# The first layer's experts add their results by accumulating indirect transfers to device memory instead of one-hot products

## Chip, cores and metric

One core of a Trainium2 chip runs the whole program; the core's engines are TensorE (PE), VectorE (DVE), ScalarE (ACT), GpSimd (POOL) and SyncE (SP), and sixteen DMA engines move data between device memory and on-chip memory. The metric is the device time of one execution in microseconds; a kernel's time is the median of several runs. The trace comes from one further execution that the hardware profiler recorded.

## The reference

Two layers work on 512 latent tokens and 256 context tokens of width 1024, in float32. Each layer mixes tokens (four groups of heads, one output projection, gated residual) and then runs 16 routed experts. The experts are what matters here:

```
def expert_choice_ffn(x, router_w, wg, wu, wd):
    bn, n, _ = x.shape
    cap = CAPACITY_FACTOR * n // N_EXPERTS
    aff = jax.nn.softmax(jnp.einsum('bnd,de->bne', x, router_w).astype(jnp.float32), axis=-1)
    gate, idx = lax.top_k(aff.transpose(0, 2, 1), cap)
    bidx = jnp.arange(bn)[:, None, None]
    xg = x[bidx, idx]
    hid = jax.nn.silu(jnp.einsum('becd,edf->becf', xg, wg)) * jnp.einsum('becd,edf->becf', xg, wu)
    o = jnp.einsum('becf,efd->becd', hid, wd) * gate[..., None].astype(x.dtype)
    return jnp.zeros_like(x).at[bidx, idx].add(o)
...
        x = x + g2 * expert_choice_ffn(...)
        if not last:
            xc = xc + cg2 * expert_choice_ffn(...)
```

Each expert chooses `cap` tokens: 64 of the 512 latent ones, 32 of the 256 context ones. A token can be chosen by several experts, but an expert lists a token once. The first layer runs the experts on both kinds of tokens with the same weights, the second layer on the latent tokens alone. Each expert has three 1024 x 1024 matrices (gate, up, down), 4 MB each, 201 MB a layer.

## The kernel before

On-chip memory is one slab of 49984 words per partition that `Arena` hands out. `Stream` (`st`) holds the weight transfers of both layers in a fixed order. It issues the next one on SP's queue as soon as less than `st.limit` words are held, so each product that frees a chunk (`st.done`) pumps the next transfer. An expert matrix is four chunks of 2048 words per partition (1024 KB, `CUTS`). `AHEAD` and `BESIDE` (lines 41 and 42) set the limit by stage and layer.

Ahead of the experts of a layer, `wout_unit` computes the output projection and adds it to the residual `X` (six tiles of 128 tokens), `rows_out` (L1397) stores the finished columns of `X` to `rows` in device memory, `willing` and `route` find each expert's tokens, and `fetch` (L1463) gathers 128 rows at a time from `rows` by an indirect transfer on GpSimd's queue: two experts' latent tokens, or four experts' context tokens. `turned` scales and transposes what was gathered.

In the first layer `experts_both` (L1804) goes through the experts. For expert e it runs `gate` of e+1, then `down` of e, then `up` of e+1, each by `both_mm` (L1647): for every chunk, `lat_mm` (L1602, 16 matmul records a chunk) and `ctx_mm` (L1610, 8 records). TensorE's order is the order written here (`in_turn`); the other engines' orders are set by a scheduler that simulates the program. `out_lat` and `out_ctx` multiply the results by the routing weights and the layer's gate, into `o`, a tile of 128 rows that two experts (latent) or four (context) fill together.

When a tile is full, `scatter(r, g)` (L1723) adds it to `X`. `mark` builds a matrix that has a one where a row of `o` belongs to a token; `o` is split into a high and a low part, and each `part` multiplies both with the one-hot matrix (L1733 and L1734, one matmul record each) and adds the bank to a 128 x 512 piece of `X` on VectorE (L1736). A latent group has 8 parts and a context group 4; with 8 and 4 groups that is 80 parts in the first layer. They wait in `todo`, and `both_mm` takes up to two of them after a chunk of weights:

```
                if c in at:
                    at[c]()
                else:
                    for _ in range(min(much, len(todo))):
                        todo.popleft()()
```

The last 12 parts follow the last expert. Then the second layer starts with the `X` that is still on the chip: `norm1` squares its rows (L717), VectorE scales them (L722), and TensorE turns them (L610). `X` is also stored to `x1` (L1923), from where the second layer reads it again before its output projection (L1290). The second layer's experts (`experts_latent`) use `scatter` too, without `todo`.

Of the kernel before, what the change touches and what calls it, by code (L numbers as in the profile page):

```python
# [28 lines left out]
NE = 16  # L29
# [10 lines left out]

AHEAD = ((16384, 20480), (16384, 24576), (28672, 40960))
BESIDE = (26624, 34816)
MORE = (4096, 8192)
# [183 lines left out]
def hybrid_kernel(ctx: ExitStack, tc: tile.TileContext, T, out):  # L227
# [35 lines left out]
    def small(n, name, dt=F32, bufs=4, p=128):  # L263
        return smp.tile([p, n], dt, name=name, tag=name, bufs=bufs)
# [248 lines left out]
    def latest(engine):  # L513
        return next(i for i in reversed(nc.cur_bb.bb.instructions) if i.engine == engine)
# [22 lines left out]
    def layer(l):  # L537
# [751 lines left out]
        for s in (slice(0, 512), slice(512, 1024)):  # L1289
            sp.dma_start(X.v[:, 0:4, s], tiles(T["x"])[:, :, s] if cx else x1.rearrange("t p f -> p t f")[:, 0:4, s])  # L1290
            if cx:
                sp.dma_start(X.v[:, 4:6, s], tiles(T["ctx"])[:, :, s])
# [104 lines left out]
        def rows_out(r, a, b):  # L1397

            sp.dma_start(rows[r][:, a:b].rearrange("(t p) f -> p t f", p=128),
                         X.v[:, 4 * r:4 * r + (4 >> r), a:b])  # L1400

        def route(lat):
# [52 lines left out]
            return icol, ii, gcol  # L1455

# [39 lines left out]
        def mark(r, g):  # L1496

            n = 512 if r == 0 else 256
            m = ohm()
            dve.tensor_scalar(m.r[:, 0:n], iota.v[:, 0:n], rt[r][0][:, g:g + 1], None, OP.is_equal)  # L1500
            return m
# [88 lines left out]
        if cx:  # L1590
            setbanks(G=[0, 1, 2], C=[3, 4], T=[5, 6, 7])
            kinds["X"] = kinds["T"]
        else:
            setbanks(G=[0], U=[1], D=[3], T=[5, 6], X=[7, 2, 4])
        OO, OC = {}, {}

# [47 lines left out]

        todo = deque()

        def both_mm(e, wn, xl, xc, at, much=2):  # L1647

            B, Cb = bank("G"), bank("C")
            for c, (k0, nk) in enumerate(CUTS):  # L1650
                w = st.get(("exp", l, e, wn, k0))
                lat_mm(B, xl(), w, k0, nk)
                ctx_mm(Cb, xc(), w, k0, nk)
                st.done(("exp", l, e, wn, k0))
                if c in at:
                    at[c]()
                else:
                    for _ in range(min(much, len(todo))):
                        todo.popleft()()
            return B, Cb  # L1660
# [31 lines left out]
        def out_lat(e, B):  # L1692
            gc = rt[0][2]
            if e % 2 == 0:
                OO[e // 2] = orr()
            o = OO[e // 2].v
            p0 = (e % 2) * 64
            for n in range(2):
                s = slice(n * 64, n * 64 + 64)
                dve.scalar_tensor_tensor(o[p0:p0 + 64, n * 512:(n + 1) * 512], B[s, :], gc[s, e:e + 1],  # L1700
                                         G2.v[s, 0, n * 512:(n + 1) * 512], OP.mult, OP.mult)

        def out_ctx(e, Cb):
            if e % 4 == 0:
                OC[e // 4] = orc()
            o = OC[e // 4].v
            gc = rt[1][2]
            p0 = (e % 4) * 32
            a, b = halves(Cb, gc[64:128, e:e + 1])
            dve.scalar_tensor_tensor(b, a, gc[0:64, e:e + 1], b, OP.mult, OP.add)  # L1710
            for n in range(2):
                s = slice(n * 32, n * 32 + 32)
                dve.tensor_tensor(o[p0:p0 + 32, n * 512:(n + 1) * 512], b[s, :],
                                  G2.v[s, 1, n * 512:(n + 1) * 512], OP.mult)

        def down(e, hT):
# [5 lines left out]

        def scatter(r, g):  # L1723

            m = mark(r, g)
            o = (OO if r == 0 else OC)[g]
            n = 512 if r == 0 else 256
            ol = o.split()

            def part(t, s, oh):  # L1730
                B = bank("X")
                lh = m.r[:, t * 128:(t + 1) * 128]
                pe.matmul(B, lh, oh.r, start=True, stop=False)  # L1733
                pe.matmul(B, lh, ol[:, s], start=False, stop=True)  # L1734
                xs = X.v[:, 4 * r + t, s]
                dve.tensor_tensor(xs, xs, B, OP.add)  # L1736

            for f in range(2):
                s, oh = slice(f * 512, (f + 1) * 512), ohr()
                act.activation(oh.r, o.v[:, s], AF.Copy)  # L1740
                dve.tensor_tensor(ol[:, s], o.v[:, s], oh.v, OP.subtract)
                for t in range(n // 128):
                    if cx:
                        todo.append(lambda t=t, s=s, oh=oh: part(t, s, oh))
                    else:
                        part(t, s, oh)

# [56 lines left out]
        def experts_both():  # L1804

            nonlocal iota, ohm, ohr
            hT, wait = {}, {}
# [17 lines left out]
            with in_turn():  # L1825
# [3 lines left out]
                for e in range(NE):  # L1829
# [14 lines left out]
                    B, Cb = both_mm(e, "down", lambda: x, lambda: y, {})  # L1844
                    while todo:
                        todo.popleft()()
# [12 lines left out]
                    if e + 1 < NE:  # L1859
# [9 lines left out]
                        B, Cb = first(e + 1, "up", spread(fs))  # L1869
                while todo:  # L1870
                    todo.popleft()()

        def experts_latent():
# [3 lines left out]
            for e in range(NE - 1):  # L1877
# [28 lines left out]
                if e % 2:  # L1906
                    scatter(0, e // 2)

# [5 lines left out]
        if not cx:  # L1914
            finish(NE - 1, hl)
        for r in (xtr, xgr, et, h1r, ht, orr, ohr, ohm) + ((xtc, h2r, hcr, htc, orc) if cx else ()):
            r.free()
        G2.free()
        ar.tight = False
        iota.free()  # L1920
# [118 lines left out]
```

## Time and profile before

| | before |
|---|---|
| median of 3 runs | 1978.82 us (1976.78 to 1978.9) |
| the profiled execution | 1984.42 us |
| its span, first to last instruction | 1982.3 us |
| TensorE matmul busy | 1825.0 us, 92% |
| VectorE busy | 897.6 us, 45% |
| ScalarE busy | 653.7 us, 33% |
| GpSimd busy | 228.4 us, 12% |
| HBM read, written | 513.40 MB, 10.52 MB |
| mean rate | 264 GB/s |

Times in rows count from the start of the span. "x" is a number of instructions, and what stands in brackets or behind an arrow is what an engine waited for before an instruction. The first layer's experts run from about 540 to 1106 us, the second layer's from about 1525 us to the end.

### The profile page before, as it was taken

The numbers are of one execution on the slowest core, as the hardware profiler recorded it, in microseconds if no ns is written. First come the engines' busy times: TensorE is split into PE (matmuls) and PEld (weight loads), VectorE is DVE, ScalarE is ACT, GpSimd is POOL, SyncE is SP. The second block draws the span as 40 slices with busy tenths as digits, with TensorE's granted clock in tenths as the row PEclk, the third lists the DMA queues.
The fourth block names the chain that finished last, engine by engine and source line by source line (L and its number), as shares of the span: only waits on it lengthen the run. The fifth ranks groups of instructions, "written<-read, shape, count | busy, mean of one in ns | idle before, by whom it ended". The sixth has DMA issues, their size and how long they took to land.

```text
span 1982.3 us, 31560 instructions
## 1 busy us (share of the span) xinstructions
PE 1825.0 (92%) x13037; PEld 1022.3 (52%) x13037; DVE 897.6 (45%) x1881; ACT 653.7 (33%) x1390; POOL 228.4 (12%) x191
## 2 busy tenths in 40 slices
PE   6999988989899999999999799998898999888888
PEld 3886787679533333333333488696694333222323
DVE  3758564533523434434434575864534233223322
ACT  2456544532322322331221345644521211111101
POOL 0432033101100000000000044132110000000000
PEclk9999999979899999999999899998998999999999
DMA  9116135532699999999998122425737999999997
GB/s 341 55 49 200 43 115 174 195 138 86 224 409 407 386 344 364 372 351 357 351 359 298 59 64 99 144 94 196 280 104 287 422 421 421 422 422 422 422 422 293
DMA packets 156542, 525.97 MB, mean 265 GB/s; under 512 B 12240, under 2 KB 42864, under 8 KB 132336
## 3 DMA queue, kind: packets, MB, share of 16 engines
q1 hardware_dynamic: 153664, 514.00, 68.2%
q0 software_dynamic: 2736, 9.97, 1.3%
q8 instruction: 102, 1.67, 0.3%
q14 instruction: 40, 0.33, 0.0%
HBM read 513.40 MB, written 10.52 MB: 264 GB/s over the span
## 4 chain that ended last, share of the span: by engine, by line
PE 33%; DMA 15%; DVE 4%; ACT 2%; issue 1%; SPq 1%; POOL 0%; ACTq 0%; DVEq 0%; POOLq 0%
PE banks L1602 15%; DMA ar<-in_exp_w_gate 4%; DMA ar<-in_exp_w_down 4%; DMA ar<-in_exp_w_up 4%; PE banks L1610 3%; PE banks L1332 2%; DMA ar<-in_w_in 2%; PE banks L633 1%; PE banks L702 1%; PE banks L644 1%; PE banks L1733 1%; PE banks L463 1%; PE banks L1734 1%; SPq L1035 1%; PE banks L1486 0%
## 5 line engine op out<-in xcount | busy, mean ns | idle before, releaser
L1602 PE MATMUL banks<-ar,ar 128*32 128x512 f32 (+1 forms) x4576 | 714.1, 598 | 32.9 <-DMA ar<-in_exp_w_down 14.0
L1602 PEld LDWEIGHTS banks<-ar,ar 128*32 128x32 f32 (+1 forms) x4576 | 194.6, 119 | 457.2 <-issue 379.0
L1610 PE MATMUL banks<-ar,ar 128*32 128x512 f32 x1536 | 201.2, 598 | 0.1
L633 PE MATMUL banks<-ar,ar 128*128 128x256 f32 x1344 | 175.8, 287 | 2.1 <-DVE ar L812 1.6
L633 PEld LDWEIGHTS banks<-ar,ar 128*128 128x128 f32 x1344 | 166.7, 193 | 7.2 <-issue 2.6
L1332 PE MATMUL banks<-ar,ar 128*128 128x256 f32 x960 | 137.7, 299 | 2.4 <-ACT ar L1228 1.3
L1332 PEld LDWEIGHTS banks<-ar,ar 128*128 128x128 f32 x960 | 125.8, 201 | 4.4 <-ACT ar L1228 2.4
L1736 DVE TENSOR_TENSOR ar<-ar,banks 128x512 f32<-128x512 f32 x136 | 87.4, 683 | 66.1 <-PE banks L1734 65.8
L1610 PEld LDWEIGHTS banks<-ar,ar 128*32 128x32 f32 x1536 | 50.8, 111 | 115.8 <-issue 107.9
L1466 POOL DMA_INDIRECT ar<-rows,icoli x19 | 18.4, 970 | 769.7 <-ACT ar L1491 455.4
L1700 DVE SCALAR_TENSOR_TENSOR ar<-banks,gcol,ar 64x512 f32<-64x512 f32 x62 | 46.5, 750 | 126.7 <-PE banks L1602 126.0
L411 ACT ACTIVATE ar<-banks 128x512 f32<-128x512 f32 x32 | 19.1, 597 | 256.3 <-PE banks L1602 256.3
L1491 ACT ACTIVATE ar<-banks,modT,modA 128x128 f32<-128x128 f32 x84 | 31.5, 458 | 169.4 <-PE banks L1483 138.4
L576 POOL TENSOR_TENSOR ar<-ar,ar 128x2048 fp32r<-128x2048 f32 x14 | 64.8, 4626 | 177.6 <-ACT ar L575 177.6
L463 PE MATMUL banks<-ar,S 128*32 128x256 f32 x768 | 66.3, 418 | 19.6 <-DMA ar<-in_ada_w 18.7
L911 ACT ACTIVATE ar<-banks,mx 128x768 f32<-128x768 f32 (+1 forms) x80 | 65.2, 819 | 31.1 <-DVE mx L908 28.5
L702 PE MATMUL banks<-ar,ar 128*128 128x512 f32 (+1 forms) x288 | 71.6, 395 | 3.8 <-DVE ar L603 2.0
L908 DVE TENSOR_REDUCE mx<-banks 128x1 f32<-128x768 f32 (+1 forms) x80 | 66.6, 846 | 15.2 <-PE banks L903 12.1
L414 DVE SCALAR_TENSOR_TENSOR ar<-banks,ar 128x512 f32<-128x512 f32 x32 | 21.9, 683 | 112.0 <-ACT ar L413 112.0
L1671 DVE TENSOR_TENSOR ar<-banks,ar 64x512 f32<-64x512 f32 x32 | 21.8, 680 | 95.1 <-ACT ar L1616 95.1
L644 PE MATMUL banks<-ar,ar 128*128 128x512 f32 (+1 forms) x288 | 62.2, 370 | 2.3 <-ACT ar L820 2.2
L1679 DVE COPY ar<-banks 128x512 f32<-128x512 f32 x32 | 22.1, 691 | 91.0 <-PE banks L1677 91.0
(343 smaller groups left out, 2541.7 us busy)
## 6 DMA issues: line engine op xcount, KB each, us to landing
ar<-in_exp_w_gate SPq DMA_DIRECT2D x128, 1024.0 KB
ar<-in_exp_w_up SPq DMA_DIRECT2D x128, 1024.0 KB
ar<-in_exp_w_down SPq DMA_DIRECT2D x124, 1024.0 KB
ar<-in_ada_w SPq DMA_DIRECT2D x96, 512.0 KB
ar<-in_w_in SPq DMA_DIRECT2D x18, 1024.0 KB
ar<-in_w_out SPq DMA_DIRECT2D x8, 1024.0 KB
ar<-in_exp_w_down SPq DMA_DIRECT2D x7, 512.0 KB
ar<-in_rpb SPq DMA_DIRECT2D x8, 384.0 KB
```

The costliest lines, as they stand in the source:

```text
L463: pe.matmul(B[32 * q:32 * q + 32, 0:n], S[:, k, :], w[:, q * n:(q + 1) * n], start=k == 0, stop=k == 7)
L576: pool.tensor_tensor(lo, raw, hi.v, OP.subtract)
L633: pe.matmul(B[:, tt * 256:(tt + 1) * 256], a.r[:, k, t * 128:(t + 1) * 128], b[:, k, :], start=n == 0, stop=n == 23)
L644: pe.matmul(B[:, 0:n1 - n0], b[:, k, c * 128:(c + 1) * 128], a.r[:, k, n0:n1], start=n == 0, stop=n == 23)
L702: pe.matmul(PS[:, t, s], x.r[:, k, t * 128:(t + 1) * 128], w, start=k == 0 and i == 0, stop=k == 7 and i == 2)
L908: dve.tensor_reduce(mx, s, AX, OP.max, negate=True)
L911: act.activation(e, s, AF.Exp, bias=mx, accum_out=sm)
L1332: pe.matmul(B, a[:, c, t * 128:(t + 1) * 128], b[:, k, :], start=i == 0, stop=i == 23)
L1602: pe.matmul(B[n * 64 + j:n * 64 + j + p, :], xt[:, k, j:j + p], w[:, k - k0, n * 512:(n + 1) * 512], start=k == 0, stop=k == 7)
L1610: pe.matmul(B[j:j + 32, :], xt[:, k, :], w[:, k - k0, n * 512:(n + 1) * 512], start=k < 2, stop=k > 5)
L1700: dve.scalar_tensor_tensor(o[p0:p0 + 64, n * 512:(n + 1) * 512], B[s, :], gc[s, e:e + 1], G2.v[s, 0, n * 512:(n + 1) * 512], OP.mult, OP.mult)
L1736: dve.tensor_tensor(xs, xs, B, OP.add)
```

## The change

The first layer keeps its residual in device memory during the experts. `x1` is replaced by `xs_`, one tensor of 512 rows and one of 256 rows. `rows_out` stores each piece to `rows` and to `xs_`, and `X` is freed after the routing. Each expert's result is now one tile of its own (64 latent rows or 32 context rows), and `give` adds it to the chosen rows of `xs_` by an indirect transfer with an add, issued on GpSimd's queue: 32 transfers. After the last expert, `X` is allocated again and loaded from `xs_` by six transfers, and the second layer's later read of `X` takes `xs_[0]`. `route` computes the row numbers that this needs. The deque, the one-hot matrices and the table `iota` of the first layer go; the limits on weights ahead rise in the first layer. The second layer's experts keep the one-hot products.

```diff
-AHEAD = ((16384, 20480), (16384, 24576), (28672, 40960))
-BESIDE = (26624, 34816)
+AHEAD = ((16384, 20480), (16384, 24576), (32768, 40960))
+BESIDE = (32768, 34816)
...
-    x1 = drp.tile([6, 128, D], F32, name="x1")
+    xs_ = [drp.tile([n, D], F32, name="xs%d" % n) for n in (NL, NCX)]
...
         def rows_out(r, a, b):
-            sp.dma_start(rows[r][:, a:b].rearrange("(t p) f -> p t f", p=128),
-                         X.v[:, 4 * r:4 * r + (4 >> r), a:b])
+            for d in (rows[r], xs_[r]) if cx else (rows[r],):
+                sp.dma_start(d[:, a:b].rearrange("(t p) f -> p t f", p=128), X.v[:, 4 * r:4 * r + (4 >> r), a:b])
...
+            to = None
+            if cx:
+                tof = small(16, "tof%d" % r, bufs=1)
+                dve.tensor_tensor(tof[0:cap], dif[0:cap], ia[0:cap], OP.add)
+                to = small(16, "to%d" % r, I32, bufs=1)
+                dve.tensor_copy(to[0:cap], tof[0:cap])
...
         rt[0] = route(True)
+        if cx:
+            X.free()
...
         def out_lat(e, B):
             gc = rt[0][2]
-            if e % 2 == 0:
+            if cx or e % 2 == 0:
                 OO[e // 2] = orr()
             o = OO[e // 2].v
-            p0 = (e % 2) * 64
+            p0 = 0 if cx else (e % 2) * 64
...
+            if cx:
+                give(0, e, o)
+
+        def give(r, e, o):
+            n = 64 >> r
+            pool.indirect_dma_start(out=xs_[r], out_offset=bass.IndirectOffsetOnAxis(
+                ap=rt[r][3][0:n, e:e + 1], axis=0), in_=o[0:n], in_offset=None, compute_op=OP.add)
...
         def out_ctx(e, Cb):
-            if e % 4 == 0:
-                OC[e // 4] = orc()
-            o = OC[e // 4].v
+            o = orc().v
...
+            give(1, e, o)
...
                     out_lat(e, B)
                     out_ctx(e, Cb)
-                    if e == 1:
-                        iota = Buf(ar, (512,))
-                        sp.dma_start(iota.v, T["iota"])
-                        ohm, ohr = Rot(ar, (512,), 2), Rot(ar, (512,), 4)
-                    if e + 1 == NE:
-                        kinds["X"][0] = [5, 6, 7, 0, 1, 2, 3, 4]
-                    if e % 2:
-                        scatter(0, e // 2)
-                    if e % 4 == 3:
-                        scatter(1, e // 4)
...
-                while todo:
-                    todo.popleft()()
+                X = Buf(ar, (6, 1024))
+                for r in range(2):
+                    for t in range(4 >> r):
+                        sp.dma_start(X.v[:, 4 * r + t], xs_[r][t * 128:(t + 1) * 128])
...
-        if l == 0:
-            for t in range(4):
-                sp.dma_start(x1[t], X.v[:, t])
```

## Rows read from the trace of the kernel before

**Rows 1.** Page, forty equal slices of the span: rate of the DMA engines.
```profile
GB/s 341 55 49 200 43 115 174 195 138 86 224 409 407 386 344 364 372 351 357 351 359 298 59 64 99 144 94 196 280 104 287 422 421 421 422 422 422 422 422 293
```
**Rows 2.** Busy time by stretch: us, engines (instructions), TensorE clock, DMA share, GB/s.
```profile
560.00:620.00 60.00, 60.00 (x535) 19.64 (x536) 22.54 (x35) 17.42 (x31) 0.94 (x1) 1.00 1.03 413
950.00:1000.00 50.00, 50.00 (x420) 16.87 (x416) 22.75 (x36) 12.35 (x22) 0.00 (x0) 1.00 0.93 335
530.00:535.00 5.00, 4.84 (x32) 1.09 (x24) 2.73 (x11) 0.88 (x3) 2.39 (x3) 0.66 0.15 23
```
**Rows 3.** Waits of weight loads (busy, idle before) and SP's queue, expert stage.
```profile
L1602 PEld LDWEIGHTS banks<-ar,ar 128*32 128x32 f32 x3024 | 92.0, 110 | 206.3 <-issue 199.7 <-DMA ar<-in_exp_w_up 1.6 <-DMA ar<-in_exp_w_down 1.2
...
SPq L365 <- PE banks L1610: 421.8, 165, 4.1
```
**Rows 4.** TensorE in order of time: start, us, line, matmuls; chunks without and with parts.
```profile
811.51 1.90 PE L1602 MATMUL banks<-ar,ar 128*32 128x512 f32 x16
...
824.39 1.90 PE L1602 MATMUL banks<-ar,ar 128*32 128x512 f32 x16
...
827.08 0.50 PE L1733 MATMUL banks<-ar,ar 128*128 128x512 f32 x1
...
828.20 1.92 PE L1602 MATMUL banks<-ar,ar 128*32 128x512 f32 x16
...
832.05 1.92 PE L1602 MATMUL banks<-ar,ar 128*32 128x512 f32 x16
```
**Rows 5.** Line L1733 from 545 to 1105.5 us: count, ns min/median/max, first and last.
```profile
L1733 PE MATMUL banks<-ar,ar x68: 387/447/504, 611.6 to 1056.8; 128*128 128x512 f32 x68
```
**Rows 6.** SP's queue in order of time: stores of rows, issues of gate weights.
```profile
511.96 0.51 SPq L1399 DMA_DIRECT2D rows<-ar  x1
...
698.45 11.71 SPq L365 DMA_DIRECT2D ar<-in_exp_w_gate  x4
...
842.54 11.71 SPq L365 DMA_DIRECT2D ar<-in_exp_w_gate  x4
```
**Rows 7.** TensorE, VectorE and ScalarE in order of time, between the two layers.
```profile
1104.65 1.04 PE L1610 MATMUL banks<-ar,ar 128*32 128x512 f32 x8
...
1104.90 1.53 DVE L1700 SCALAR_TENSOR_TENSOR ar<-banks,gcol,ar 64x512 f32<-64x512 f32 x2 [11.86 <-PE banks L1602]
...
1112.96 0.63 ACT L717 ACTIVATE ar<-ar 128x512 f32<-128x512 f32 x1
...
1117.26 0.16 DVE L719 TENSOR_REDUCE ss<-ss1h 128x4 f32<-128x8 f32 x1
...
1120.75 2.74 DVE L722 TENSOR_SCALAR ar<-ar,n10y 128x1024 f32<-128x1024 f32 x4
```
**Rows 8.** Transfers: gathers to landing; software queue, 540 to 600 us; X's store; rope's load.
```profile
DMA to landing us min/median/max: 4.2/7.3/9.1
...
q0 software_dynamic: 320, 1.13, 5.5%
...
1113.78 2.89 SPq L1923 DMA_DIRECT2D x<-ar  x4
...
1115.00:1120.00 5.00, 0.96 (x3) 0.48 (x3) 3.84 (x10) 4.91 (x17) 0.00 (x0) 0.77 0.97 388
...
1089.57 2.00 DMA ar<-in_rope
```
**Rows 9.** VectorE and TensorE in order of time, last expert of the first layer.
```profile
1091.69 0.76 DVE L662 TENSOR_TENSOR ar<-ar,cl 128x256 f32<-128x256 f32 x2 [0.15 <-DMA ar<-in_rope]
...
1093.10 0.46 PE L1686 MATMUL banks<-c,ar 64*128 64x64 f32 x4 [2.88 <-DVE ar L1834]
1093.49 3.37 PE L1602 MATMUL banks<-ar,ar 128*32 128x512 f32 x16
```
**Rows 10.** GpSimd in order of time: gathers.
```profile
532.26 1.34 POOL L1466 DMA_INDIRECT ar<-rows,icoli  x1 [22.09 <-DVE ar L1500]
...
726.95 0.94 POOL L1466 DMA_INDIRECT ar<-rows,icoli  x1 [69.20 <-ACT ar L1491]
```

More of the change, by code (lines that the diff above doesn't have):

```diff
@@ L2 @@
 import re
-from collections import deque
 from contextlib import ExitStack, contextmanager
@@ L1289, in layer @@
         for s in (slice(0, 512), slice(512, 1024)):
-            sp.dma_start(X.v[:, 0:4, s], tiles(T["x"])[:, :, s] if cx else x1.rearrange("t p f -> p t f")[:, 0:4, s])
+            sp.dma_start(X.v[:, 0:4, s], tiles(T["x"] if cx else xs_[0])[:, :, s])
             if cx:
@@ L1452, in route @@
             dve.tensor_tensor(gcol, va, vb, OP.max)
+            to = None
[4 more added lines that the diff above has]
+                dve.tensor_copy(to[0:cap], tof[0:cap])
             for b_ in rbuf[r] + [afl[r]]:
                 b_.free()
-            return icol, ii, gcol
+            return icol, ii, gcol, to
         rt, marks = {}, {}
@@ L1496, in mark @@
         def mark(r, g):
-            n = 512 if r == 0 else 256
             m = ohm()
-            dve.tensor_scalar(m.r[:, 0:n], iota.v[:, 0:n], rt[r][0][:, g:g + 1], None, OP.is_equal)
+            dve.tensor_scalar(m.r, iota.v, rt[r][0][:, g:g + 1], None, OP.is_equal)
             return m
@@ L1591, in layer @@
             setbanks(G=[0, 1, 2], C=[3, 4], T=[5, 6, 7])
-            kinds["X"] = kinds["T"]
         else:
             setbanks(G=[0], U=[1], D=[3], T=[5, 6], X=[7, 2, 4])
-        OO, OC = {}, {}
+        OO = {}
         def lat_mm(B, xt, w, k0, nk):
@@ L1643, in first_mm, with both_mm @@
             return B
-        todo = deque()
-        def both_mm(e, wn, xl, xc, at, much=2):
+        def both_mm(e, wn, xl, xc, at):
             B, Cb = bank("G"), bank("C")
@@ L1656, in both_mm @@
                     at[c]()
-                else:
-                    for _ in range(min(much, len(todo))):
-                        todo.popleft()()
             return B, Cb
@@ L1712, in out_ctx @@
                 s = slice(n * 32, n * 32 + 32)
-                dve.tensor_tensor(o[p0:p0 + 32, n * 512:(n + 1) * 512], b[s, :],
+                dve.tensor_tensor(o[0:32, n * 512:(n + 1) * 512], b[s, :],
                                   G2.v[s, 1, n * 512:(n + 1) * 512], OP.mult)
+            give(1, e, o)
         def down(e, hT):
@@ L1721, in down, with scatter @@
             out_lat(e, B)
[L1723 to L1727, printed above, removed]
+        def scatter(g):
+            m, o = mark(0, g), OO[g]
             ol = o.split()
@@ L1734, in part @@
                 pe.matmul(B, lh, ol[:, s], start=False, stop=True)
-                xs = X.v[:, 4 * r + t, s]
-                dve.tensor_tensor(xs, xs, B, OP.add)
+                dve.tensor_tensor(X.v[:, t, s], X.v[:, t, s], B, OP.add)
             for f in range(2):
@@ L1741, in scatter @@
                 dve.tensor_tensor(ol[:, s], o.v[:, s], oh.v, OP.subtract)
[L1742 to L1746, printed above, removed]
+                for t in range(4):
+                    part(t, s, oh)
         def finish(e, hT):
@@ L1804, in experts_both @@
         def experts_both():
-            nonlocal iota, ohm, ohr
+            nonlocal X
             hT, wait = {}, {}
@@ L1844, in experts_both @@
                     B, Cb = both_mm(e, "down", lambda: x, lambda: y, {})
-                    while todo:
-                        todo.popleft()()
                     out_lat(e, B)
                     out_ctx(e, Cb)
-                    if e == 1:
-                        iota = Buf(ar, (512,))
-                        sp.dma_start(iota.v, T["iota"])
-                        ohm, ohr = Rot(ar, (512,), 2), Rot(ar, (512,), 4)
-                    if e + 1 == NE:
-                        kinds["X"][0] = [5, 6, 7, 0, 1, 2, 3, 4]
-                    if e % 2:
-                        scatter(0, e // 2)
-                    if e % 4 == 3:
-                        scatter(1, e // 4)
                     if e + 1 < NE:
@@ L1869, in experts_both @@
                         B, Cb = first(e + 1, "up", spread(fs))
-                while todo:
-                    todo.popleft()()
+                X = Buf(ar, (6, 1024))
+                for r in range(2):
+                    for t in range(4 >> r):
+                        sp.dma_start(X.v[:, 4 * r + t], xs_[r][t * 128:(t + 1) * 128])
         def experts_latent():
@@ L1906, in experts_latent @@
                 if e % 2:
-                    scatter(0, e // 2)
+                    scatter(e // 2)
         hl = ohr = None
@@ L1915, in layer @@
             finish(NE - 1, hl)
-        for r in (xtr, xgr, et, h1r, ht, orr, ohr, ohm) + ((xtc, h2r, hcr, htc, orc) if cx else ()):
+        for r in (xtr, xgr, et, h1r, ht, orr) + ((xtc, h2r, hcr, htc, orc) if cx else (ohr, ohm, iota)):
             r.free()
@@ L1919, in layer @@
         ar.tight = False
-        iota.free()
-        if l == 0:
-            for t in range(4):
-                sp.dma_start(x1[t], X.v[:, t])
         state["x"] = X
```

1 line of the change is left out of this document (removed).

## The prediction

> **What bounds the kernel now.** I read the slices of the page first, then tables of stretches, then who waits for whom, then the instructions in order of time. In the slices [rows 1] two stretches move over 290 GB/s without a break: slices 12 to 22 (first layer's experts) and the last nine (second layer's, 422 GB/s). The change edits the first. There TensorE and the DMA engines both look full, and the whole prediction hangs on which one is the limit.
>
> The tables [rows 2] settle it. From 560 to 620 us the core moves 413 GB/s with the DMA share at 1.03; from 950 to 1000 us it moves 335 GB/s and the share still reads 0.93. So the share says little; the bytes say that later the engines were asked for less than they can do. TensorE is busy 50.00 of 50.00 us there. The waits agree [rows 3]: between 545 and 1105 us TensorE's weight loads at L1602 lost 2.8 us to expert weights (1.6 + 1.2), while the queue that issues those weights waited 421.8 us in 165 waits for TensorE's L1610 to free a buffer. The loads follow TensorE. What leaves TensorE's instruction stream there shortens the stage, until the DMA engines become the limit.
>
> **The change part by part.**
>
> *One-hot products removed inside the stage.* Before, `todo` puts two parts behind a weight chunk, each with two matmuls (L1733, L1734). A chunk without parts starts 2.576 us after the one before it: (824.39 - 811.51) / 5 [rows 4]. With two parts it takes 832.05 - 828.20 = 3.85 us. A pair of parts therefore costs 1.274 us: four matmuls and the change of array shape around them. L1733 runs 68 times in the stage [rows 5], 34 pairs: 34 x 1.274 = **43.3 us off TensorE**. As a check: four experts take 842.54 - 698.45 = 144.1 us by the issues of their `gate` weights [rows 6], 36.0 us each; they hold 20 parts, so 10 pairs or 12.7 us, and 32.8 us per expert is left. VectorE and ScalarE lose L1736, L1741, L1740 and L1500 beside this; they were not the limit, so this counts nothing.
>
> *Is there DMA capacity for it?* All 10 chunks that the limit of 20480 words allows had landed by 535 us: the engines were nearly idle from 530 to 535 us at 23 GB/s [rows 2]. The layer has 192 chunks of 1.0486 MB, so 182 are to come, 190.8 MB. Eleven gathers of 0.525 MB add 5.8 MB. At 413 GB/s that is 476 us. New are the accumulating transfers, per expert 96 rows of 4 KB = 0.393 MB. No row of this trace is an accumulating one. The nearest are the gather's packets, 165 ns each (5.5% of 16 engines over 60 us for 320 packets), and a plain store of 2.1 MB at 388 GB/s [rows 8]. With six rows per engine and expert, one pass costs 1.0 us per expert, a read and a write of the destination 2.0 us; below nothing is excluded, since bytes are added. I take 2.0 us, over 15 experts 30 us. The last chunk then lands at 535 + 476 + 30 = 1041 us at the earliest. TensorE, 43.3 us sooner, needs it at 1105.7 - 43.3 - 2.6 = 1059.8 us. So the weights stay ahead and the 43.3 us is kept whole, with 19 us of cover. The cover ends at a = (1059.8 - 1011) / 15 = 3.3 us per expert. Sixteen chunks of room (32768 words, after `X.free()`) instead of 13 or 14 help to keep it.
>
> The Trainium skill, page "Collectives: The Full Stack", section "The bandwidth ceiling: the fold count and why AG ≠ RS ≠ AR", says that an add in the DMA engine costs a second source read rather than time for the adding, which halves the rate. By it the price is an estimated 1.9 us per expert, not the 1.0 us of a plain pass: the sum stays, but the cover is 20 us, not the 34 us of a plain pass, which speaks for rival 1. No row here shows an add.
>
> *Queues.* GpSimd's queue gets two transfers per expert, 0.9 to 1.3 us each as the gathers [rows 10]; each waits for VectorE's product and for the transfer before it to the same tensor, 33 us earlier. Behind them stand only the gathers. A gather waits until the transposes free its buffer and is then issued, some 70 us after the last [rows 10] and as long before its own use; its landing takes up to 9.1 us [rows 8], and it may now be issued a whole expert later without being missed. `orr` and `orc` have one buffer: VectorE writes the next after 33 us, far more than a landing. If that cover went, VectorE would stand behind a landing, some 3 us of TensorE's time at each expert at worst.
>
> *Before the stage.* `rows_out` stores everything twice: 3 MB more, five more issues on SP. Its last, 0.5 MB, goes out near 512 us [rows 6], in front of the last chunks of `up`: 1.3 us, of which iota's 0.26 MB (no longer loaded there) gives back half. The gather at 532.26 us waits for VectorE's routing [rows 10], so this costs nothing; without that cover, 1 us.
>
> *The end of the stage.* Before: last product of `down` ends at 1104.65 + 1.04 = 1105.7 us, twelve parts follow beside VectorE's adds, and L722 of the second layer starts at 1120.75 us [rows 7]: 15.1 us. After: VectorE's two products end 0.7 us behind; the last accumulate must be issued and land, taken at the gather's shortest 4.2 us as the engines are idle then (bounds 2.0 us, the landing of rope's 128 KB [rows 8], and 9.1 us); then 2.1 MB of X must come back. The store of the same bytes lasted from 1113.78 to about 1120 us [rows 8], so 7 us with its completion. Only after the fourth tile can the last squares run (L717, 0.63 us [rows 7] and a short read of the sum, so 0.75 us apart; two to five of them), and eight small instructions of statistics follow, which I estimate at 2.2 us; with other work between them they took 3.5 us before, from L719 to L722. Together 0.8 + 4.2 + 7 + 1.5 + 2.2 = 15.7 us, or 19.3 us with five squares and 3.5 us. I take 17.6: **2.5 us more**, bounds -1.6 and +9. The store to x1 went beside other work and gives nothing.
>
> The Trainium skill, "DMA: Bandwidth & Descriptors", section "Anatomy of one DMA — SWDGE (gpsimd) path", gives 2.0 us and the bytes at 436 GB/s for such a transfer, an estimate of 2.6 us for the last accumulate; by that the end costs 0.9 us more, not 2.5. The trace's gathers, at least 4.2 us, stand against it.
>
> *By chance.* VectorE's queue holds the second layer's L662 before L1834 of the last expert, and L662 waits for rope's load: TensorE idles 2.88 us and runs its next 16 matmuls in 3.37 us instead of 1.90 us [rows 4, 9]. With other buffers this may go (4.4 us more gain) or stay; I count nothing.
>
> **Sum.** -43.3 + 2.5 = -40.8 us. The profiled execution took 1984.4 us (span 1982.3 us and 2.1 us around it), so 1943.6 us; the median of the runs is 5.6 us below that execution: 1978.8 - 40.8 = **1938 us**. The second layer shifts as a block, since its own weight loads start from its own buffers.
>
> **Rivals.**
>
> 1. *The DMA engines become the limit of the stage.* If an expert's accumulates cost them a > 3.3 us, the end of the stage moves by 15 us per us of a. For it: before, weights alone filled 413 GB/s where TensorE asked for 407 (1.0486 MB per 2.576 us). Against: a would have to be over three times the price of plain rows. At a = 5: 535 + 476 + 75 + 2.6 = 1088.6 us, 17 us gained less 2.5, 1964 us; range 1943 to 1977.
>
> 2. *Slower: each accumulated row holds its engine for a round trip to memory.* Place: the 16 engines in the same stage; price: at the 2.0 us of an isolated load, six rows are 12 us per expert, the last product ends at 535 + 476 + 180 + 2.6 = 1194 us, 88 us later than before, with the end 2070 us. It decides from a = 6.0 us, 1.0 us a row. For it: an add must read before it writes. Against: gathered rows of the same size cost 165 ns, with many in flight.
>
> 3. *The seam between the layers costs more.* Landing at 9.1 us beside other loads, gathers that stop ScalarE's queue (as the L1478 waits do now), reload behind other loads on SP: 5 to 15 us, 1943 to 1953 us.
>
> **Chances.** The forecast 0.66 (alone 1930 to 1946: the rope stall gone, or the end at its upper bound); rival 1 0.16, rival 3 0.07, rival 2 0.08; 0.03 that gain and losses cancel. About 0.2% (4 us) is what can be told from no change. Faster 0.87, same 0.03, slower 0.10. To hold eight in ten, the range takes the forecast, rival 3 and most of rival 1: 1930 to 1962 us.
>
> **What would show it.** Right: two expert chunks always 2.58 us apart, an expert every 32.8 us, the queue of loads still waiting for L1610, the last `down` product near 1062 us, L722 17 us behind it, GpSimd with 32 more transfers. Wrong: weight loads on TensorE waiting for in_exp_w by tens of us, with GB/s under 400 (rivals 1 and 2); packets of the software queue far over 330 ns (rival 2); L722 more than 22 us behind the last product (rival 3).

## The result, and the profile after

The changed kernel takes 1954.2 us (median, 1950.7 to 1958.3) against 1978.9 us for the kernel before: ratio 0.9874, 95% interval [0.9853, 0.9896], 24.6 us less. A second measurement (after_again) gives 1954.2 us and, to the kernel before beside it, 0.9855 [0.9828, 0.9881]. The forecast was 1938 us, 40.8 us less: the sign and the range held, but some 16 us of the forecast gain are missing. The profiled execution took 1950.7 us (span 1948.9), the shortest of its four, where that of the kernel before (1984.4 us) was longer than any of the four in its median; the second pair of profiles, 1978.8 and 1954.2 us of span, lies 24.6 us apart as the medians do.

The forecast's picture of the stage can be seen in the new trace. The stretches move 401 and 402 GB/s now, against 413 and 335 before [rows 2]: both near the 413 that was the most in the stage before, so the DMA engines are now asked for much from start to end. Columns as in [rows 2].

```profile
560.00:620.00 60.00, 60.00 (x556) 19.18 (x552) 18.68 (x29) 16.16 (x29) 6.58 (x5) 1.00 1.03 401
950.00:1000.00 50.00, 46.67 (x420) 14.23 (x412) 13.01 (x21) 9.35 (x17) 2.74 (x2) 0.97 1.03 402
```

TensorE's chunks in order of time, to be set beside [rows 4]: no parts between them.

```profile
811.19 1.90 PE L1607 MATMUL banks<-ar,ar 128*32 128x512 f32 x16
...
821.49 1.90 PE L1607 MATMUL banks<-ar,ar 128*32 128x512 f32 x16
```

(821.49 - 811.19) / 4 = 2.575 us, as predicted. But the table of stretches shows 46.67 of 50 busy us in the second stretch, where it was 50.00 before. The waits of TensorE (us in total, times, longest) and of SP's queue over the stage name the cause:

```profile
PE banks L1607 <- DVE ar L1700: 8.0, 2, 4.7
...
SPq L364 <- PE banks L1615: 221.7, 113, 7.4
```

The queue of weights still waits for TensorE (half as much as in [rows 3]), and not the other way round. New is the first line: twice, TensorE waits for VectorE's L1700, the eviction of an expert's `down` product (it scales the product and so moves it out of its bank). In order of time, TensorE at both waits, its clock behind the first (columns as in [rows 2]), and VectorE ahead of the first:

```profile
928.99 1.04 PE L1615 MATMUL banks<-ar,ar 128*32 128x512 f32 x8
934.75 3.64 PE L1607 MATMUL banks<-ar,ar 128*32 128x512 f32 x16 [4.71 <-DVE ar L1700]
938.16 1.56 PE L1615 MATMUL banks<-ar,ar 128*32 128x512 f32 x8
939.55 1.89 PE L1607 MATMUL banks<-ar,ar 128*32 128x512 f32 x16
...
972.49 2.85 PE L1607 MATMUL banks<-ar,ar 128*32 128x512 f32 x16 [3.33 <-DVE ar L1700]
...
976.78 1.90 PE L1607 MATMUL banks<-ar,ar 128*32 128x512 f32 x16
```
```profile
934.70:944.70 10.00, 9.95 (x73) 2.63 (x76) 3.41 (x5) 3.11 (x5) 3.08 (x2) 0.77 1.03 378
```
```profile
906.78 0.74 DVE L1715 SCALAR_TENSOR_TENSOR ar<-banks,gcol,ar 64x512 f32<-64x512 f32 x1 [1.08 <-ACT ar L1621]
...
920.03 0.69 DVE L1834 TENSOR_TENSOR ar<-ar,ar 64x512 f32<-64x512 f32 x1
924.39 0.69 DVE L1679 COPY ar<-banks 128x512 f32<-128x512 f32 x1 [3.68 <-PE banks L1677]
931.19 0.69 DVE L413 SCALAR_TENSOR_TENSOR ar<-banks,ar 128x512 f32<-128x512 f32 x1 [6.11 <-ACT ar L412]
932.58 0.69 DVE L1665 TENSOR_TENSOR ar<-ar,banks 128x512 f32<-128x512 f32 x1 [0.69 <-ACT ar L414]
933.18 1.51 DVE L1700 SCALAR_TENSOR_TENSOR ar<-banks,gcol,ar 64x512 f32<-64x512 f32 x2
```

L1715 evicts the context half of the same expert at 906.78 us, so its product is complete by then. L1700 runs only at 933.18. VectorE was idle for 3.68 and 6.11 us in between, and the transfer that had read `orr` before was issued at 892.45 us and landed within 7.4 us (6.8 to 7.4 us between 880 and 945 us). Over the whole stage VectorE idled ahead of L1700 for TensorE's products alone, never for a transfer:

```profile
its engine sat idle before it (us, times) until:
  PE banks L1607: 25.5, 7
```

Nothing that the trace shows kept L1700 of expert e back but its place: it stands behind the sigmoid products L413 and L1665 of the `gate` of expert e+2. The bank that it should empty is the one that the next `down` needs, three products later (G has three banks), and that is the product that waits. The price is 4.71 + 3.33 us of waiting and the chunk behind each, which runs partly at the lower of the clock's two levels (a mean of 0.77 granted from 934.7 to 944.7 us): 939.55 - 934.75 = 4.80 us, and 4.29 us at the other, in place of 2.58. Together 8.0 + 3.9 = 11.9 us.

Between the layers, in order of time, and in the chain of what ended last (start, us, what):

```profile
1072.73 1.04 PE L1615 MATMUL banks<-ar,ar 128*32 128x512 f32 x8
1092.40 0.16 DVE L718 TENSOR_REDUCE ss<-ss1h 128x4 f32<-128x8 f32 x1 [15.64 <-ACT ar L716]
1095.49 2.74 DVE L721 TENSOR_SCALAR ar<-ar,n10y 128x1024 f32<-128x1024 f32 x4 [0.24 <-DVE n10y L405]
```
```profile
1074.79 8.30 DMA xs<-ar,to
...
1083.97 5.58 DMA ar<-xs
```

The last product ends at 1073.8 us, some 11 us later than the forecast's 1062, and L721 (L722 before) starts 21.7 us behind it; before it was 15.1 us [rows 7], forecast 17.6. The 32 accumulates of the layer land in these times (the chain's 8.30 goes on to the issue of the reload):

```profile
DMA to landing us min/median/max: 5.5/7.1/8.1
```

All profiles cut at the same points (us). "Routed" is the end of the cast of the latent indices (`icoli`); then the wait until the stage's first gather is issued; the time from "routed" to the end of the last `down` product; from there to L721; from L721 to the end of the span.

```
kernel           routed   to gather  stage   seam   rest    median
before            531.4     0.9      574.3   15.1   861.6   1978.9
before_again      536.8     1.0      570.6   15.1   856.4
changed           531.6     2.7      542.2   21.7   853.4   1954.2
after_again       538.5     2.8      542.9   18.8   854.0   1954.2
two_tiles         533.0     2.7      531.5   18.2   855.3   1939.7
two_tiles_again   531.8     2.4      530.6   18.7   850.5   1939.7
bound             531.1     2.4      530.2   19.0   855.6   1943.7
pinned            533.3     3.2      539.3   19.3   855.3   1950.6
no_give           533.9     1.6      529.0    7.4   853.4   1933.1
plain_two         534.9     1.9      530.3   16.7   853.3   1936.3
twice_pin         531.4     2.5      544.0   33.5   852.9   1967.0
store_pool        538.7     0.3      526.4   18.5   854.2   1937.2
```

"Routed" comes at 531 to 535 us or at 537 to 539 us, in both kernels; single executions differ by that much. Two profiles of one kernel also differ by up to 3.7 us in the stage (before), 2.9 in the seam (changed) and 5.2 in the rest (before), so only larger differences count by themselves. The medians come from four measurements, in which the kernel before took 1978.9 us (changed), 1984.2 (after_again, two_tiles, pinned, no_give), 1980.0 (bound, plain_two, twice_pin, before_again) and 1984.8 (store_pool, two_tiles_again); across them the ratios are the safer comparison.

### The profile page after: what moved, and what is told of

It reads as the page before. It is cut to its first block, busy times and chain, and to the rows that moved or that the text cites. A ratio compares the mean times of both kernels' runs of the same rounds, so it can differ in the third digit from the quotient of the medians.

```text
span 1948.9 us, 31192 instructions
## 1 busy us (share of the span) xinstructions
PE 1772.1 (91%) x12877; PEld 995.0 (51%) x12877; DVE 827.3 (42%) x1769; ACT 638.1 (33%) x1366; POOL 271.8 (14%) x226
## 4 chain that ended last, share of the span: by engine, by line
PE 60%; DMA 19%; issue 9%; DVE 6%; ACT 4%; SPq 1%; POOL 0%; DVEq 0%; POOLq 0%; ACTq 0%
PE banks L1607 21%; PE banks L1331 6%; PE banks L1615 6%; PE banks L632 5%; DMA ar<-in_exp_w_up 4%; DMA ar<-in_exp_w_gate 4%; PE banks L643 3%; DMA ar<-in_w_in 3%; PE banks L701 3%; DMA xs<-ar,to 2%; PE banks L462 2%; DMA ar<-in_exp_w_down 2%; PE banks L1040 1%; DMA ar<-in_ada_w 1%; PE banks L924 1%
## 5 line engine op out<-in xcount | busy, mean ns | idle before, releaser
L632 PEld LDWEIGHTS banks<-ar,ar 128*128 128x128 f32 x1344 | 168.2, 194 | 7.2 <-issue 2.6
L1331 PEld LDWEIGHTS banks<-ar,ar 128*128 128x128 f32 x960 | 125.3, 200 | 3.7 <-ACT ar L1227 2.4
L1708 POOL DMA_INDIRECT xs<-ar,to x32 | 45.9, 1436 | 425.1 <-DVE ar L1700 405.6
L1700 DVE SCALAR_TENSOR_TENSOR ar<-banks,gcol,ar 64x512 f32<-64x512 f32 x62 | 46.4, 748 | 92.3 <-PE banks L1607 91.7
L413 DVE SCALAR_TENSOR_TENSOR ar<-banks,ar 128x512 f32<-128x512 f32 x32 | 21.9, 685 | 132.1 <-ACT ar L412 132.1
L701 PEld LDWEIGHTS banks<-ar,ar 128*128 128x128 f32 x288 | 51.8, 197 | 17.6 <-DVE ar L586 2.8
```

Of the source, the lines that this page charges most:

```text
L632: pe.matmul(B[:, tt * 256:(tt + 1) * 256], a.r[:, k, t * 128:(t + 1) * 128], b[:, k, :], start=n == 0, stop=n == 23)
L701: pe.matmul(PS[:, t, s], x.r[:, k, t * 128:(t + 1) * 128], w, start=k == 0 and i == 0, stop=k == 7 and i == 2)
L1331: pe.matmul(B, a[:, c, t * 128:(t + 1) * 128], b[:, k, :], start=i == 0, stop=i == 23)
L1708: pool.indirect_dma_start(out=xs_[r], out_offset=bass.IndirectOffsetOnAxis(ap=rt[r][3][0:n, e:e + 1], axis=0), in_=o[0:n], in_offset=None, ...
```

## The experiments

**after_again.** The changed kernel, unaltered.

> The changed kernel once more, unaltered, for its second profile and a closer time. Both theories: 1952 to 1956 us. If the two waits of TensorE's banks for VectorE's L1700 (4.7 us at 934 us and 3.3 us at 972 us of the first profile) belong to the program's order, they come back at the same two places; if they were one execution's accident, they don't. The place in the second layer where the first profile gained some 7 us over the kernel before (no 4.4 us wait for in_dftl, no half clock behind it) shows whether it comes back too.

1954.2 us (1951.1 to 1958.3). The wait for L1700 came back to the digit (8.0 us, 2 times, longest 4.7), the stage with it (542.9 us). It belongs to the program. The second layer's wait for in_dftl is absent again, and it took 854.0 us.

**two_tiles.** The accumulates' sources have two tiles in turn.

```diff
-        orr = Rot(ar, (1024,), 1) if cx else None
-        orc = Rot(ar, (1024,), 1) if cx else None
+        orr = Rot(ar, (1024,), 2) if cx else None
+        orc = Rot(ar, (1024,), 2) if cx else None
```

> The changed kernel, but the experts' results have two tiles in turn (orr and orc) in place of one; the work and the transfers are the same, and in the program VectorE's eviction of an expert's down product (L1700) then stands ahead of its context half and of the next expert's h1 again, as in the kernel before. Theory A (the order slipped: with one tile the eviction is put ever later among VectorE's instructions, since it is taken to wait for the transfer of the expert before, and it holds a bank of products that the expert after next needs): no wait of TensorE for L1700 in the stage, last down product at 1064 to 1066 us in place of 1073.8, time 8 to 10 us less than the changed kernel, 1944 to 1946. Theory B (the transfers themselves are late or take the queue's time, whatever the order): the same time as the changed kernel, 1952 to 1956, last down product 1072 to 1075.

1939.7 us, ratio 0.9781 [0.9752, 0.9809] to the kernel before: 14.5 us under the changed kernel, more than expected. In the built program all L1700 stand ahead of L1715 and of the next h1 again; in the changed kernel this is so for six experts, and from the seventh on L1700 stands later, latest at the eleventh and twelfth, where TensorE waits. The same expert's VectorE in this trace:

```profile
906.58 1.51 DVE L1700 SCALAR_TENSOR_TENSOR ar<-banks,gcol,ar 64x512 f32<-64x512 f32 x2 [3.17 <-PE banks L1607]
908.16 0.74 DVE L1715 SCALAR_TENSOR_TENSOR ar<-banks,gcol,ar 64x512 f32<-64x512 f32 x1
```

From 545 us to the end of the stage TensorE waits once, 2.1 us at the rope load. The last product ends at 1064.5 us, and the chain between the layers is:

```profile
1065.50 4.85 DMA xs<-ar,to
1070.40 3.80 DMA ar<-xs
```

Repeated beside store_pool as **two_tiles_again**:

> The run two_tiles once more, unaltered, beside store_pool on the same chip: 1937 to 1942 us, stage from the first gather to the last product 528 to 529 us, seam 18 to 20 us, no wait of TensorE for L1700.

1939.7 us again, 0.9782 [0.9755, 0.9809], stage 530.6, seam 18.7.

**pinned.** One tile, but h1 may not pass the evictions of the expert before (`od` is VectorE's last instruction of `out_ctx`).

```diff
-                    dve.tensor_tensor(h1, a1, B, OP.mult)
+                    with tc.issue_after(od) if e else ExitStack():
+                        dve.tensor_tensor(h1, a1, B, OP.mult)
```

> The changed kernel with one tile each as it is, but the order of VectorE is bound: an expert's h1 product may not stand ahead of the evictions of the expert before it (L1700 and those of its context half). Theory A: the same gain as with two tiles, or most of it (the eviction can still slip behind the context half's and one silu product, a few hundred ns each): last down product 1064 to 1067 us, 1944 to 1947 us. If one tile costs by a real wait for its transfer on the chip and not by the order, no gain: 1952 to 1956 us. Theory B: no gain either.

1950.6 us: 3.6 us less, not 8 to 10. The wait moved. L1700 still stood behind the silu products and h2, which weren't bound, and h1 was now kept back behind it: TensorE's transposes of h1 (L1677) waited for it, 5.7 us at once, at the last expert:

```profile
PE banks L1677 <- DVE ar L1834: 7.4, 4, 5.7
```

**bound.** One tile, and the whole order of two_tiles written out.

```diff
-                    dve.tensor_tensor(h1, a1, B, OP.mult)
-                    dve.tensor_tensor(h2, a2, whole(Cb), OP.mult)
+                    with tc.issue_after(od) if e else ExitStack():
+                        dve.tensor_tensor(h1, a1, B, OP.mult)
+                        dve.tensor_tensor(h2, a2, whole(Cb), OP.mult)
...
                     out_lat(e, B)
-                    out_ctx(e, Cb)
+                    od = latest(mybir.EngineType.DVE)
+                    with tc.issue_after(od):
+                        out_ctx(e, Cb)
+                    od = latest(mybir.EngineType.DVE)
```

> The changed kernel with one tile each as it is; two bounds in the program put VectorE's instructions of an expert in the order of the run two_tiles (eviction L1700, then the context half's L1715 and L1718, then the next h1 and h2), all of them, where the run pinned bound h1 alone and left h2 and the context half free to pass the eviction. Theory A (only the place in VectorE's order cost the stage its 9 us): 1938 to 1942 us as with two tiles, last down product 28 to 30 us past the rope load's stall as there, 1064 to 1066 us, no wait of TensorE for L1700. Rival A2 (a tile that waits on the chip for its transfer): the eviction waits for the transfer of the expert before and time stays at 1950 to 1955.

The stage takes 530.2 us, with one tile, as with two (531.5 and 530.6); TensorE's only wait behind 545 us is for h2, at the rope load:

```profile
PE banks L1686 <- DVE ar L1835: 1.5, 1, 1.5
```

For three experts L1700 still stands behind a gather's products (L1498), some 8 us late, and TensorE does not wait. VectorE idles ahead of L1700 for products of TensorE alone here too. So in this execution it is the order, and no wait for a transfer on the chip. The times spread more than those of two_tiles and miss what was expected (1943.7 us median, 1937.6 to 1948.5; ratio 0.9828 [0.9798, 0.9858] against 0.9781 [0.9752, 0.9809]). The profiled execution was the shortest of the four, so its trace cannot tell where the others lose up to 11 us; that the bound order gives back all that two tiles give is shown for the stage and not for the time.

**no_give.** The accumulates left out; the experts' results are not added.

```diff
         def give(r, e, o):
-            n = 64 >> r
...
+            return
```

> The changed kernel without its accumulating transfers in the first layer: the experts' results are computed and evicted and not added to the tokens; the reload of X stays. Both theories expect the order of VectorE as before the change and no wait for L1700. Theory A: the stage ends as with two tiles, to within 1.5 us (the transfers cost the stage nothing by themselves), 1064 to 1066 us, and the seam loses the 8.3 us in which the last transfer lands: last down product to L721 13 to 14 us in place of 21.7. Time 1935 to 1938. Theory B: the stage alone already gives 8 us over two_tiles, so 16 us or more between this and two_tiles.

1933.1 us. TensorE does not wait for L1700, with one tile. The stage is 2 us shorter than that of two_tiles, 1 us of it ahead of the first gather: the accumulates are hidden in it but for that. The seam is 7.4 us, not the 13 to 14 that were expected and less than before the change, since nothing keeps the reload of X back; it runs ahead of the last product. Chain and VectorE:

```profile
1056.04 6.84 DMA ar<-xs
```
```profile
1070.24 2.74 DVE L721 TENSOR_SCALAR ar<-ar,n10y 128x1024 f32<-128x1024 f32 x4 [0.24 <-DVE n10y L405]
```

So the wait for the last accumulate, with the reload that must follow it, costs the seam 18.2 - 7.4 = 10.8 us in these profiles, more than twice the 4.85 us of its landing in two_tiles. The medians lie 6.6 us apart; no_give's profiled execution (1925.3 us) was 7 us shorter than any other of it.

**plain_two.** two_tiles with the addition left out of the transfers (`compute_op=OP.add` removed): rows are overwritten.

> Two tiles in turn as in the run two_tiles, but the transfers write the rows and add nothing (left out: the tokens' old values and the sum over experts). Theory A: an accumulated row of 4 KB costs a DMA engine some 326 ns (worked out from the share of the queue of indirect transfers, two traces); a written one should cost as much as a gathered one, some 155 to 170 ns, so about 1.0 us of 16 engines per expert in place of 1.95. Since two_tiles hides the accumulates, the stage ends the same to within 1 us; the seam loses what the add takes of the last landing, 1 us at most. Time 1937 to 1940. Rival (the add is what holds the stage back): over 5 us faster than two_tiles.

1936.3 us (ratio 0.9783, two_tiles 0.9781), stage 530.3 us, seam 16.7 us, 1.5 to 2.0 under two_tiles where 1 at most was expected. The software queue from 700 to 1000 us (packets, MB, share of 16 engines), first in no_give with the gathers alone, then in plain_two, then in two_tiles:

```profile
q0 software_dynamic: 720, 2.62, 2.2%
```
```profile
q0 software_dynamic: 1872, 6.16, 5.1%
```
```profile
q0 software_dynamic: 1872, 6.16, 8.1%
```

Nine experts lie in it, 864 rows: (5.1 - 2.2)% x 300 x 16 / 864 = 0.161 us a written row, (8.1 - 2.2)% x 300 x 16 / 864 = 0.328 us an accumulated one; per expert 0.97 and 1.97 us of the 16 engines. The add doubles the price. GpSimd itself takes 890 ns for a plain one and 1391 ns for an accumulating one (medians), all hidden.

**twice_pin.** two_tiles with every accumulate issued twice, the order bound as in bound.

> Two tiles in turn and VectorE's order bound as in two_tiles, but every accumulating transfer is issued twice (the results are added two times). It doubles the cost in DMA time from some 1.95 to 3.9 us per expert. The prediction's sum says that the lead of the weights covers up to 3.3 us: theory A: 0.6 us x 15 experts over it, so the last experts wait for weights and the last down product comes some 9 us later than in two_tiles (1070 to 1076 us), the seam 1 to 2 us longer, time 1947 to 1953 us. Rival (the DMA engines have more room than that): only the seam, 1940 to 1943. Rival (each transfer holds GpSimd or its queue a round trip): the chunks of the stage spread from the start on, over 1955.

1967.0 us. In the stage theory A was right: the last product ends at 1075.4 us, and TensorE waits for weights (by tile, us in total, times, longest):

```profile
PE banks L1607 <- DMA ar<-in_exp_w_gate: 8.8, 12, 2.0
...
PE banks L1607 <- DMA ar<-in_exp_w_up: 1.5, 3, 0.9
```

10.3 us in all, none of it before 800 us, so the lead of the weights is used up first; the rival that GpSimd or its queue is held wanted a loss from the start, though its time (over 1955) is what came. The software queue from 700 to 1000 us:

```profile
q0 software_dynamic: 3280, 10.49, 15.4%
```

Ten experts lie in it: (15.4 - 2.2)% x 300 / 10 = 3.96 us of the 16 engines per expert, and (3.96 - 3.3) x 15 = 9.9 us were to come. The seam was missed by far, 33.5 us. VectorE, and the chain:

```profile
1084.07 0.76 DVE L661 TENSOR_TENSOR ar<-ar,cl 128x256 f32<-128x256 f32 x2 [19.60 <-DMA ar<-in_rope]
1084.74 1.51 DVE L1700 SCALAR_TENSOR_TENSOR ar<-banks,gcol,ar 64x512 f32<-64x512 f32 x2
```
```profile
1086.53 4.57 DMA xs<-ar,to
...
1091.37 4.68 DMA xs<-ar,to
```

With the queue of loads late, rope's load was issued at 1074.4 us in place of 1049.2; L661 of the second layer stands ahead of the last L1700, and it held that eviction 9 us beyond the end of its product. Then two landings came one behind the other.

**store_pool.** two_tiles, and the 2 KB store that the first gather waits for goes out by GpSimd's queue.

```diff
-            sp.dma_start(rows[r][:, D:].rearrange("(t p) f -> p t f", p=128), rs[:, :, None])
+            (pool if cx and r == 0 else sp).dma_start(rows[r][:, D:].rearrange("(t p) f -> p t f", p=128), rs[:, :, None])
```

> Two tiles in turn as in the run two_tiles, and the 2 KB store of the latent tokens' norm factors (rows<-n20y, L1394), for whose landing the first gather of the stage waits, goes out by GpSimd's queue in place of SP's, where 1 MB loads of weights stand ahead of it. Theory: in two_tiles the store is issued at 520.97 us and lands 14 us later, and VectorE has the indices at 533.0; with nothing ahead of it in its own queue it lands in 5 to 9 us, as the indirect transfers do, so the gather waits for VectorE alone and issues 2 to 3 us earlier against the first transfers of the stage (533.0 to 533.5 on the time axis of two_tiles); everything behind it shifts: 1936 to 1938 us, 2 to 3 us under two_tiles. Rival: the store shares the 16 DMA engines with the weights wherever it is issued, and 512 pieces of 4 bytes take their turns behind the same 1 MB loads: no gain, 1938 to 1941.

GpSimd in two_tiles and the store in its chain, then GpSimd in store_pool:

```profile
535.72 0.95 POOL L1471 DMA_INDIRECT ar<-rows,icoli  x1 [23.56 <-DMA rows<-n20y]
```
```profile
520.97 13.88 DMA rows<-n20y
```
```profile
522.26 0.83 POOL L1394 DMA_DIRECT2D rows<-n20y  x1 [4.37 <-DVE n20y L405]
538.94 1.44 POOL L1471 DMA_INDIRECT ar<-rows,icoli  x1 [15.85 <-ACT ar L414]
```

The store lands in 6.2 us, and the gather is issued 0.3 us after the indices in place of 2.4 to 2.7. The stage from "routed" is 526.4 us, the shortest of all; half of the 4 to 5 us under two_tiles lies ahead of the gather, and what made the other half was not traced. Time 1937.2 us (ratio 0.9763 [0.9734, 0.9793]) against 1939.7 beside it: the right size, but within the noise of the times.

**before_again.** The kernel before, unaltered.

> The kernel before once more, unaltered, for a second profile. In its first profile the second layer took 861.6 us from its first use of X to the end of the span, and in the five others 853.4 to 855.3: the difference stood at one 4.4 us wait for in_dftl at 1369 us and the half clock behind it. If that belongs to this kernel (its place in time against the loads), it comes back, and 6 us of the gain are made there; if it was one execution's, the second layer takes 853 to 856 us here too. The stage from the first gather to the last product should take 573.4 us again to within 1 us.

One time, 1981.0 us. The wait for in_dftl comes back (TensorE, in order of time):

```profile
1369.56 1.01 PE L1145 MATMUL banks<-ar,ar 128*128 128x1 f32 x4 [4.47 <-DMA ar<-in_dftl]
```

It belongs to the kernel before: 4.4 and 4.5 us in its two profiles, none in the two of the changed kernel, 1.3 to 2.3 us in the eight variants. The load is issued 4.4 to 5.0 us before these products in both kernels (1364.55 us here, 1336.89 in the changed kernel, whose products follow at 1341.73 without a wait). The second layer took 856.4 us here, not 861.6: the granted clock behind the wait was 0.83 over 20 us, and 0.66 in the first profile. So 2 to 8 us of the gain are made in the second layer. That this wait makes them is argued and not shown: the variants that wait 1.3 to 2.3 us for the load take no longer there (850.5 to 855.6 us) than the changed kernel. The expectation for the stage was missed: 569.6 us from the gather, not 573.4; where the 3.8 us lie is open.

## Why the prediction was right, and where it failed

- *34 pairs of parts off TensorE, 43.3 us*: right. From 574.3 and 570.6 us the stage falls to 531.5, 530.6 and 530.2 in two_tiles, its repeat and bound, where VectorE's order is kept: 39 to 44 us. In the changed kernel it falls by 28 to 32.
- *"So the weights stay ahead and the 43.3 us is kept whole"*: the step that failed, and by its neighbour: "`orr` and `orc` have one buffer: VectorE writes the next after 33 us, far more than a landing." The landing is short indeed (5.5 to 8.1 us), and L1700 never waits for it. But I read the single tile only as a wait on the chip, and took VectorE's order of before as given. With one tile and accumulates on it, the program put out with L1700 ever later, and at two experts it stood behind the silu of expert e+2. That took 11 to 12 us of the 43.3 (542.2 and 542.9 against 530.2 to 531.5). Two tiles, or the order bound with one, give them back in the stage. Why the planner places it late was not measured; that it does so with one tile, and does not without accumulates or with two tiles, is what the built programs show.
- *Cost of an accumulate, 2.0 us per expert*: right, 1.97 (1.95 in the changed kernel's own trace, less the kernel before's gathers: (7.5 - 2.3)% x 300 / 8 experts). The Trainium skill's "Collectives: The Full Stack", section "The bandwidth ceiling: the fold count and why AG ≠ RS ≠ AR", by which the add of a reduce-scatter costs a second source read, fits the trace better than the rows of plain transfers did: 0.328 us a row against 0.161 without the add.
- *Cover up to 3.3 us per expert*: borne out at its two sides. At 1.97 nothing waits; at 3.96 TensorE waits 10.3 us, near the 9.9 of the sum. No run keeps the old limits on weights ahead, so what the raised ones add to the cover stays open.
- *The first gather "waits for VectorE's routing, so this costs nothing"*: wrong by 1.8 us (2.7 us after the indices, before 0.9). The copies to `xs` push the 2 KB store back in SP's queue, from 517.2 to 519.2 us, and its landing, 13.9 us after the issue in two_tiles, no longer comes before the indices do. The cover was next to nothing: in before_again the chain already goes through that landing (14.85 us from 522.17 us), 0.3 us behind the indices. The forecast had the price (1 to 1.3 us) and the wrong cover.
- *Seam +2.5 us*: too small. +3.1 to +3.9 in two_tiles and its like, +3.7 and +6.7 in the two profiles of the changed kernel. The landing was 4.85 us in two_tiles, near the 4.2 taken, and 8.30 and 5.42 in the two profiles of the changed kernel. A 1 MB load of in_w_in went out 1.0 us ahead of it in both (1073.84 and 1081.47 us), so that load alone does not make the difference. The first tile of X was back 3.6 to 4.0 us after the first issue of the reload, and ScalarE waited 0.3 us at most for a later one. What I missed is behind it: with X there nearly at once, ScalarE has nearly all twelve squares still to do and not the last two to five; in two_tiles 1082.65 - 1074.38 = 8.3 us from the first square to L721, against 3.7 to 7.3 in the forecast. The Trainium skill's "DMA: Bandwidth & Descriptors", section "Anatomy of one DMA — SWDGE (gpsimd) path", from which I had estimated 2.6 us for the landing, is not borne out here: no accumulate landed in under 5.5 us in the changed kernel, nor in under 3.6 in two_tiles. Without the add, on the nearly idle engines at the end of the stage in plain_two, the last two landed in 2.6 and 3.2 us.
- *Rivals.* 1 (DMA becomes the limit) is refuted for one accumulate and shown for two. 2 (a round trip per row) is refuted: 0.328 us, not 2. 3 (a dearer seam) holds in part, 1 to 4 us over the forecast.
- *"By chance"*: the stall at the rope load stayed, 2.1 us of waiting in the changed kernel, 2.9 before.
- *"The second layer shifts as a block"*: not quite, and in the change's favour: the rest is 2 to 8 us shorter, and its wait for in_dftl went. Which of the edits moved that load against its use was not tried.
- *Sum.* The forecast ratio was 1938.0 / 1978.8 = 0.979; two_tiles has 0.978. The forecast was that of the change with the order kept, with a seam 1 us dearer and a second layer some us cheaper than in its sum: that the ratios agree so closely is in part luck. So is that the range held the changed kernel's 1954.2 us: it reached to 1962 for rivals 1 and 3, and the lost 11 to 12 us of the stage belong to neither.

The lowest median of a version that adds everything is store_pool's, 1937.2 us, 17 us under the changed kernel; it can't be told from two_tiles beside it.

## What to carry to other kernels

When a buffer's reader becomes a transfer, compare the order of the writer's engine in the built program before and after, and not only the waits: an instruction can be put late though the chip never waits there, and an eviction that is late holds a bank that a later product needs (here the third one on). A second small tile was the cure here, and for the stage the order bound in full; a bound on one instruction only moved the wait. A small store that others wait for is better kept from behind megabytes of weights on one queue (13.9 us to land, 6.2 on another).

## What the runs showed of the hardware that was not expected

- An accumulating indirect transfer costs the DMA engines twice a plain one (0.328 against 0.161 us per 4 KB row), but its landing differs by less: 6.9 us median in two_tiles, 6.1 in plain_two.
- A 2 KB store of 4-byte pieces took 13.9 us to land on the queue of the weights (two_tiles) and 6.2 us on GpSimd's (store_pool), while loads of weights ran on the first.
- A wait of TensorE cost 1.7 to 2.2 us beyond itself, since the matmuls behind it ran slower: behind waits of 2.1 us (two_tiles, rope), 3.3 and 4.7 us (changed kernel) the next chunk took 4.29, 4.29 and 4.80 us in place of 2.58. The granted clock was 0.83 and 0.77 of full on average in the 10 us behind the last two.
